# Experts of the first layer store their outputs as rows of a table, and the second layer gathers two rows for each token

## The chip, the core and the metric

One core of a Trainium2 chip runs the kernel. The metric is the device time of one execution in microseconds (us). The kernel before has a median of 1223.6 us over three runs (1219.67 to 1224.37).

## The reference

A two-layer diffusion backbone works on 512 latent tokens and 256 context tokens, each of 1024 numbers. Layer 0 mixes tokens by gated linear attention beside dense attention, layer 1 by windowed attention (128 tokens to each side, and the context). Behind each mixer stands a mixture of 16 experts, two of which are chosen for each token. The part that matters here, cut down:

```
x, ctx = x + gate2 * mixer(...)             # layer 0, then layer 1
tok  = concat(modulate(x), modulate(ctx))   # layer 0: 768 tokens; layer 1: the 512 latent ones
combine[n, e] = weight of expert e for token n, nonzero for two e
f    = sum over e of (silu(tok @ Wg[e]) * (tok @ Wu[e]) * combine[:, e]) @ Wd[e]
x    = x   + gate5_latent  * f[:512]        # gate5: one row of 1024 numbers each
ctx  = ctx + gate5_context * f[512:]        # layer 0 alone
```

Layer 1 begins with a root-mean-square norm and a modulation of x and ctx and their projection to queries, keys and values.

## The kernel before

**Tokens and experts.** The 768 tokens are six tiles of 128 rows. Tiles 4 and 5 are the context; they are worked on first (order 4, 5, 0, 1, 2, 3; "tile 0" and so on below count in this order). A router gives every token and choice a place among the 128 slots of its expert (`CAP`). Where an expert has more tokens than slots, a branch after the experts (`overflow`) does the rest; it is not taken here. `H` in device memory holds the modulated tokens, `F` the residual stream, written by the mixer.

**One expert.** POOL gathers its 128 rows of `H` by an indirect DMA into `hg` (L1026). PE transposes them (`hgtr`), ACT and DVE split them into a high and a low part (`hh`, `hlo`). The weights stream in on SP's hardware queue (L112) into a ring of buffers, are split by ACT (`whi`, L205) and DVE (`wlo`, L206), and PE makes three products for each (`eacc`). ACT and DVE form `sg`, PE transposes it (`hidtr`), ACT copies it (`th`, L1068), and PE makes the expert's output in two halves of 512 columns (`yacc`). An expert's `yacc` stands one step behind its `eacc`. The order on each engine follows the order in which `between`, `expert_up` and `expert_down` call each other.

**What becomes of an output in layer 0.** DVE makes the gate row of each slot, context or latent (`expert_gate`, L1076), and multiplies both halves of `yacc` by it (L1091). POOL adds the rows into `F` by an indirect DMA with addition (L1093); rows of empty slots lie out of bounds and are skipped, so 768 x 2 = 1536 of the 2048 slot rows are written. Layer 1's experts do the same into the output, with one gate row for all.

**The start of layer 1.** The tiles of `F` are loaded by SP (`xc`, L1665; three buffers). The first load waits for all additions into `F`. The other tiles, and the query weights (`uq`, 4 units of 512 KB in two loads each, `wraw<-in_od_w_in_dram`, L317), wait until the first load has landed. For each tile ACT squares and sums, POOL takes the power (`ss`, L211, L212), DVE scales (`xn`, L781), PE transposes (`xtr`), ACT and DVE make the halves of the modulated tile (`tf`, L795 and L797) and split it (`hT` and `hL`; `hT1c` and `hL1c` for the context). PE then projects it (`acc`): 256 columns for keys and values (weights loaded earlier) for each tile, and 512 columns of queries for the latent tiles with `uq`, which ACT and DVE split first (`whi`, `wlo`, 128x1024).

Of the kernel before, what the change touches and what calls it, by code (L numbers as in the profile page):

```python
# [18 lines left out]
P = 128  # L19
D = 1024  # L20
# [127 lines left out]
class K:  # L148
# [65 lines left out]
    def setup(self):  # L214
        nc = self.nc
        self.cpool = self.pool("cpool")
        self.cb = self.cpool.tile([P, NCONST], F32, name="cb")
        self.ident = self.cst("ident")
        self.mhalf = self.cpool.tile([P, 32], F32, name="mhalf")
        nc.vector.memset(self.mhalf, -0.5)  # L220
        self.ring = self.pool("ring", bufs=5)
        self.dram = self.pool("dram", space=DRAM)
        self.rowstack = ExitStack()
        self.rowp = self.pool("rowp", stack=self.rowstack, side="right")
        self.modT = [self.cpool.tile([P, 2, 16], F32, name=f"modT{l}") for l in range(2)]
        self.modD = [self.dram.tile([2, 6 * D], F32, name=f"modD{l}") for l in range(2)]

# [676 lines left out]
    def route_tiles(self, l, T, wk):  # L904
# [4 lines left out]
        r["ws"], r["idx"] = t("ws", [P, 16]), t("idx", [P, 2, 16], U32)  # L909
        r["ctx"] = t("ctx", [P, 16])  # L910
        r["counts"] = t("counts", [P, 2, P], F32R)
# [5 lines left out]
    def route_group(self, wk, pt, ix, L, n0, G, r):  # L917
# [42 lines left out]
        if last:  # L960

            r["done"] = V.tensor_scalar(r["idx"][:, 0, :], ix[:, :16], float(NOROW), float(T * P - 1), op0=ALU.add, op1=ALU.min).ins
            V.tensor_scalar(r["idx"][:, 1, :], ix[:, :16], float(NOROW), None, op0=ALU.add)
            V.tensor_scalar(r["ctx"], ix[:, :16], float(SEQ - NOROW), None, op0=ALU.is_ge)

# [41 lines left out]
    def route(self, wk, r, l):  # L1007

        V = self.nc.vector
        T = r["T"]  # L1010
        keep = wk.tile([P, 2, T], F32, name=f"keep{l}")
        V.tensor_scalar(keep, r["pos"], float(CAP), None, op0=ALU.is_ge)
# [57 lines left out]

    def expert_gate(self, e, gate, isctx, wk):

        if len(gate) == 1:
            return gate[0]
        y = wk.tile([P, D], F32, tag="y", name="y", bufs=2)
        self.nc.vector.scalar_tensor_tensor(y, gate[1], isctx[:, e:e + 1], gate[0], op0=ALU.mult, op1=ALU.add)  # L1076
        return y

    def expert_down(self, e, st, h, F, rows, gate, idx, wk, pm, adds):

        nc = self.nc
        y = wk.tile([P, D], F32, tag="yo", name="yo", bufs=2) if rows == SEQ else gate
# [9 lines left out]
        x = EORDER[e]  # L1092
        i = nc.gpsimd.indirect_dma_start(F, bass.IndirectOffsetOnAxis(ap=idx[:, 1, x:x + 1], axis=0), y, None,  # L1093
# [145 lines left out]
def emit(ctx, tc, A, out, dbg=None, upto=99):  # L1239
# [298 lines left out]
    def experts(l, T, F, st, r):  # L1538
# [20 lines left out]
        with s2:  # L1559
# [11 lines left out]
            sg = None  # L1571
            hid, slot_gate, adds = {}, {}, []

            def between(e, sg):
# [3 lines left out]
                if e == 0:  # L1578
                    k.slot_weights(r, pt)
                else:  # L1580
                    slot_gate[e - 1] = k.expert_gate(EORDER[e - 1], gate, r["ctx"], ew)
                if e + 1 < NEXP:
# [4 lines left out]
            for e in range(NEXP + 1):  # L1587
# [4 lines left out]
                if e > 0:  # L1592
                    k.expert_down(e - 1, st, hid[e - 1], F, T * P, slot_gate[e - 1], idx, ew, pm, adds)
        return n
# [19 lines left out]
    op = k.pool("oT1", stack=so)  # L1614
    oh, ol = op.tile([P, 8, SEQ], F32R, name="oh1"), op.tile([P, 8, SEQ], F32R, name="ol1")
    s0, sh, sn, sp = ES(), ES(), ES(), ES()
# [30 lines left out]
    with ES() as s1:  # L1647
# [14 lines left out]
        first = None  # L1662
        for i in order:
# [44 lines left out]
    def q_rest():  # L1708
        yield from k1
        qacc = pm.tile([P, 2, 256], F32, name="qacc")  # L1710
        for v in range(2):
            u = k.proj_units(hk, [(0, k.cols(W, 768, 256))], 256, w=256) if v else u1
            for i in range(4):
                acc = qacc[:, i % 2, :]
                for j in range(4):
# [3 lines left out]
                    yield  # L1719

    V = lambda kt, v: zk[:, kt, 128 + 64 * v:192 + 64 * v]
    blocks = []
# [48 lines left out]
```

## Time and profile before

| | |
|---|---|
| median of three runs | 1223.6 us (1219.67 to 1224.37) |
| the profiled execution | 1226.32 us, of which the span is 1224.6 us |
| mean granted clock of TensorE | 0.952 |
| busy share PE / DVE / ACT / POOL | 90% / 65% / 50% / 19% |
| chain that ended last | PE 57%, DVE 8%, DMA 8%, ACT 4%, POOL 4%, issue 3% |

All times in the rows below are microseconds from the start of the span, or durations, unless the view says ns. PE is the matrix engine (PEld its weight loads), DVE, ACT and POOL the vector, scalar and GpSimd engines; SP only issues DMAs. A name such as `F<-y,idx` is output<-input. The chain of waits follows the work that ended last back from what released it. Layer 0's experts run from about 565 to 731 us; layer 1's projections from there to about 801.

### The profile page before, as it was taken

The page shows a single profiled execution, that of the slowest core. Times are in us where ns is not written, and L with a number is a line of the kernel's source. Part 1 is how long each engine was busy: PE and PEld are TensorE (multiplying, and loading weights), DVE is VectorE, ACT ScalarE, POOL GpSimd, SP SyncE. Part 2 cuts the span into 40 slices and gives each one's busy share as a digit, 9 for nine tenths or more (in the row PEclk, how much of TensorE's full clock was granted, in tenths as well). Part 3 has the DMA queues.
Part 4 walks back from the last instruction along what each step waited for, and adds up shares of the span by engine and source line. Part 5 has one row for each costly group of instructions (what it writes and reads, how often), then busy time and mean ns, then how long its engine had stood idle before and what let it go on. Part 6 is the DMA issues. An engine that isn't in the chain of part 4 may idle for free.

```text
span 1224.6 us, 21495 instructions
## 1 busy us (share of the span) xinstructions
PE 1105.9 (90%) x7986; PEld 817.4 (67%) x7986; DVE 791.5 (65%) x1613; ACT 614.4 (50%) x1266; POOL 237.2 (19%) x252
## 2 busy tenths in 40 slices
PE   5999998998889989978999885989989996899996
PEld 2688887665556667866777654877766785677773
DVE  2532355677677753668888765677688447677773
ACT  3533644555466652216555536467588522555551
POOL 1000011224222000031222221331230004133321
PEclk8999999999899999978999996999999998899998
DMA  9711102776464428658999977012041374998992
GB/s 319 238 47 60 35 11 82 272 235 214 170 224 131 148 86 262 223 207 283 348 326 333 325 233 227 12 44 70 1 138 36 108 256 174 314 318 289 297 308 46
DMA packets 106251, 228.11 MB, mean 186 GB/s; under 512 B 21429, under 2 KB 30391, under 8 KB 106132
## 3 DMA queue, kind: packets, MB, share of 16 engines
q1 hardware_dynamic: 94324, 197.15, 48.0%
q0 software_dynamic: 9216, 22.09, 7.3%
q10 hardware_dynamic: 2592, 7.34, 1.5%
q8 instruction: 67, 1.10, 0.4%
q14 instruction: 52, 0.43, 0.1%
HBM read 210.60 MB, written 27.41 MB: 194 GB/s over the span
## 4 chain that ended last, share of the span: by engine, by line
PE 57%; DVE 8%; DMA 8%; ACT 4%; POOL 4%; issue 3%; SPq 1%; POOLq 0%; ACTq 0%; DVEq 0%
PE eacc L172 11%; PE acc L172 11%; PE yacc L172 7%; PE ptr L184 4%; DMA wraw<-in_exp_w_up_dram 4%; PE pv L172 4%; PE sc L172 4%; PE modps L172 3%; PE qacc L172 3%; PE hgtr L184 2%; PE co L172 2%; PE lg L172 2%; POOL rq L435 1%; DVE wlo L206 1%; PE h2tr L184 1%
## 5 line engine op out<-in xcount | busy, mean ns | idle before, releaser
L206 DVE TENSOR_TENSOR wlo<-wraw,whi 128x1024 fp32r<-128x1024 f32 (+2 forms) x184 | 210.2, 1156 | 80.9 <-ACT whi L205 71.0
L205 ACT CAST whi<-wraw 128x1024 fp32r<-128x1024 f32 (+2 forms) x184 | 181.1, 994 | 145.4 <-PE eacc L172 94.8
L172 PE MATMUL eacc<-whi,hh 128*128 128x512 f32 x256 | 119.7, 468 | 0.0
L172 PE MATMUL yacc<-wraw,th 128*128 128x512 f32 x256 | 115.2, 593 | 1.1 <-ACT th L1068 1.1
L172 PE MATMUL eacc<-whi,hlo 128*128 128x512 f32 x256 | 102.6, 401 | 0.0
L172 PE MATMUL eacc<-wlo,hh 128*128 128x512 f32 x256 | 102.2, 399 | 0.0
L172 PE MATMUL acc<-whi,hT 128*128 128x512 f32 (+2 forms) x256 | 91.8, 359 | 4.8 <-ACT hT L205 4.8
L172 PE MATMUL acc<-wlo,hT 128*128 128x512 f32 (+2 forms) x256 | 88.8, 347 | 0.5 <-DVE wlo L206 0.4
L184 PE MATMUL ptr<-cb,P 128*128 128x128 f32 x480 | 77.5, 284 | 12.8 <-ACT PT L540 6.4
L172 PE MATMUL acc<-whi,hL 128*128 128x512 f32 (+2 forms) x256 | 88.4, 345 | 0.0
L172 PEld LDWEIGHTS yacc<-wraw,th 128*128 128x128 f32 x256 | 48.2, 189 | 49.9 <-issue 44.1
L184 PEld LDWEIGHTS ptr<-cb,P 128*128 128x128 f32 x480 | 52.9, 141 | 38.8 <-ACT PT L540 9.9
L172 PE MATMUL modps<-mw,csT 128*32 128x512 f32 (+1 forms) x448 | 64.8, 571 | 10.4 <-DMA mw<-in_mod_w_dram 6.1
L172 PE MATMUL sc<-Kst,Qh 128*128 128x512 f32 (+2 forms) x192 | 64.7, 344 | 3.6 <-ACT P L544 3.5
L504 DVE CUSTOM_DVE_ANT_0 sc<-sc,mk,sink 128x512 f32<-128x512 f32 (+1 forms) x64 | 56.2, 882 | 16.8 <-PE sc L172 14.6
L540 ACT COPY PT<-ptr 128x512 f32<-128x512 f32 x96 | 56.1, 587 | 16.8 <-PE ptr L184 15.7
L172 PE MATMUL pv<-PT,z_k 128*64 128x256 f32 x480 | 63.7, 389 | 0.0
L172 PEld LDWEIGHTS eacc<-whi,hh 128*128 128x128 f32 x256 | 49.9, 195 | 14.5 <-issue 6.7
L172 PEld LDWEIGHTS eacc<-wlo,hh 128*128 128x128 f32 x256 | 50.0, 195 | 14.3 <-issue 6.7
L172 PEld LDWEIGHTS acc<-whi,hT 128*128 128x128 f32 x256 | 49.4, 193 | 14.5 <-ACT hT L205 5.2
L172 PE MATMUL sc<-Kst,Ql 128*128 128x512 f32 (+2 forms) x192 | 56.5, 316 | 1.1 <-DVE Ql L206 1.1
L172 PEld LDWEIGHTS eacc<-whi,hlo 128*128 128x128 f32 x256 | 49.3, 192 | 11.9 <-DVE hlo L206 0.7
(331 smaller groups left out, 2530.7 us busy)
## 6 DMA issues: line engine op xcount, KB each, us to landing
mw<-in_mod_w_dram SPq DMA_DIRECT2D x80, 512.0 KB
wraw<-in_exp_w_gate_dram SPq DMA_DIRECT2D x128, 256.0 KB
wraw<-in_exp_w_up_dram SPq DMA_DIRECT2D x128, 256.0 KB
wraw<-in_exp_w_down_dram SPq DMA_DIRECT2D x64, 512.0 KB
mw<-in_mod_w_dram SPq DMA_DIRECT2D x32, 256.0 KB
wraw<-in_ev_w_in_dram SPq DMA_DIRECT2D x12, 512.0 KB
wraw<-in_od_w_in_dram SPq DMA_DIRECT2D x20, 256.0 KB
wraw<-in_od_w_out_dram SPq DMA_DIRECT2D x16, 256.0 KB
```

The lines of the kernel that those rows point to most:

```text
L172: return self.nc.tensor.matmul(out, lhsT=l, rhs=r, start=start, stop=stop)
L184: self.nc.tensor.transpose(out, in_, self.ident[:in_.shape[0], :in_.shape[0]])
L205: self.nc.scalar.copy(hi, src)
L206: self.nc.vector.tensor_tensor(lo, src, hi.bitcast(F32), op=ALU.subtract)
L435: nc.gpsimd.tensor_tensor(rq[:, 0, :], ms, self.mhalf[:, :8], op=ALU.pow)
L504: nc.vector.tensor_tensor_reduce(sc[:, lo:lo + L], sc[:, lo:lo + L], mask, rq[:, 1, h:h + 1], sink[:, 1, h:h + 1], ALU.add, ALU.min, mx[:, ...
L540: (nc.scalar.copy if a0 == 0 else nc.vector.tensor_copy)(u2["PT"][:, a0:a0 + m, j2, :], t[:, 0:m, :])
```

## The change

Layer 0's experts no longer gate and no longer add. Each expert's 128 output rows are copied out of PSUM unscaled (half 0 by ACT, half 1 by DVE) and written by a plain DMA on POOL's software queue to rows 128x to 128x+127 of a table `Y` in device memory, for all slots. The router works out for each token the two rows of `Y` that hold its outputs (`slot`; tokens over `CAP` point to a row of zeros). At the start of layer 1, POOL gathers two rows of `Y` for each token of a tile, and DVE adds the two, multiplies by the gate row and adds the result to the loaded tile of `F`; the four latent tiles are written back to `F` by ACT's queue. The two buffers for each of two tiles are the memory in which the attention output is kept later. What was released by the landing of the first `xc` load (the other tiles' loads and `uq`) is now released by the landing of tile 0's second gather, and so are tile 1's gathers. The gathers of tile t+2 wait until DVE has read tile t's buffers. Layer 1's experts keep their gate and their addition.

```diff
+        self.slot = self.cpool.tile([P, 2, 6], U32, name="slot")
+        self.Y = self.dram.tile([NEXP * P + 1, D], F32, name="Y")
...
+        if l == 0:
+            by = wk.tile([P, 2, T, 16], F32, name="slotby")
+            sl, far = (wk.tile([P, 2, T], F32, name=n) for n in ("slotf", "slotn"))
+            V.tensor_tensor(by, r["OH"], self.cst("iota")[:, None, None, 0:16].to_broadcast([P, 2, T, 16]), op=ALU.mult)
+            V.tensor_reduce(sl, by, axis=AX.X, op=ALU.add)
...
-    def expert_gate(self, e, gate, isctx, wk):
...
-        self.nc.vector.scalar_tensor_tensor(y, gate[1], isctx[:, e:e + 1], gate[0], op0=ALU.mult, op1=ALU.add)
...
+        x = EORDER[e]
+        if gate is None:
+            for n in range(2):
+                (nc.scalar.copy, nc.vector.tensor_copy)[n](y[:, n * 512:(n + 1) * 512], ya[n])
+            nc.gpsimd.dma_start(self.Y[x * P:(x + 1) * P, :], y)
+            return
...
-        gate = [k.row(cp, l, t, 5, f"g5_{t}") for t in range(T // 2 - 1)]
-        if T == 6:
-            with tc.issue_after(r["dve"]):
-                nc.vector.tensor_tensor(gate[1], gate[1], gate[0], op=ALU.subtract)
...
+        def fetch_y(t):
+            yi[t] = [spare(oh, 2 * (t % 2) + j) for j in range(2)]
+            return [nc.gpsimd.indirect_dma_start(yi[t][j], None, k.Y, bass.IndirectOffsetOnAxis(ap=k.slot[:, j, t:t + 1], axis=0)).ins
+                    for j in range(2)]
+        spare = lambda o, j: o[:, j, :]
+        for t, i in enumerate(order):
+            m = 0 if i < 4 else 1
             xi[i] = wk.tile([P, D], F32, tag="xc", name="xc", bufs=3)
-            d = nc.sync.dma_start(xi[i], F[i * P:(i + 1) * P, :]).ins
+            ds = [nc.sync.dma_start(xi[i], F[i * P:(i + 1) * P, :]).ins]
+            if m not in g5:
+                g5[m] = spare(ol, m)
+                nc.sync.dma_start(g5[m], k.modD[0][m, 5 * D:6 * D].partition_broadcast(P))
+            if t < 2:
+                ds += fetch_y(t)
             if first is None:
-                first = d
+                first = ds[2]
             else:
-                k.after(d, first)
+                for d in ds:
+                    k.after(d, first)
...
+                t = order.index(i)
+                ya, yb = yi[t]
+                nc.vector.tensor_tensor(ya, ya, yb, op=ALU.add)
+                nc.vector.tensor_tensor(ya, ya, g5[m], op=ALU.mult)
+                nc.vector.tensor_tensor(xi[i], xi[i], ya, op=ALU.add)
+                if t + 2 < 6:
+                    fetch_y(t + 2)
                 k.norm_hT(wk, pt, xi[i], AB1[:, m, :], k.modT[1][:, m, 0:8], *parts(i))
+                if i < 4:
+                    nc.scalar.dma_start(F[i * P:(i + 1) * P, :], xi[i])
```

The order of instructions moves with it. DVE before, from the end of the branch behind layer 0's experts (`C_q` to `S_k` are rotary tables):

```order
L1105 UNCONDITIONAL_BRANCH x2
L353 TENSOR_TENSOR C_q<-cs,gb_q 128x256
L359 TENSOR_TENSOR S_q<-cs,gb_q 128x8x16 x2
L353 TENSOR_TENSOR C_k<-cs,gb_k 128x256
L359 TENSOR_TENSOR S_k<-cs,gb_k 128x8x16 x2
L781 TENSOR_SCALAR xn<-xc,ss 128x1024 x2
L797 TENSOR_SCALAR tf<-xtr,AB_4100,modT_70 128x128 x4
L781 TENSOR_SCALAR xn<-xc,ss 128x1024
L206 TENSOR_TENSOR hL1c<-tf,hT1c 128x4x128 x2
```

DVE now, from the first instruction that does any work behind that branch (L1703 to L1705 are the three new operations of a tile; `early_oh` holds gathered rows, `early_ol` the gate rows):

```order
L1703 TENSOR_TENSOR early_oh_7861<-early_oh_7861 128x1024
L1704 TENSOR_TENSOR early_oh_7861<-early_oh_7861,early_ol_7862 128x1024
L1705 TENSOR_TENSOR xc<-xc,early_oh_7861 128x1024
L1703 TENSOR_TENSOR early_oh_7861<-early_oh_7861 128x1024
L1704 TENSOR_TENSOR early_oh_7861<-early_oh_7861,early_ol_7862 128x1024
L1705 TENSOR_TENSOR xc<-xc,early_oh_7861 128x1024
L206 TENSOR_TENSOR wlo<-wraw,whi 128x1024 x2
L783 TENSOR_SCALAR xn<-xc,ss 128x1024
L206 TENSOR_TENSOR wlo<-wraw,whi 128x1024 x2
L799 TENSOR_SCALAR tf<-xtr,AB_4102,modT_70 128x128 x4
L206 TENSOR_TENSOR hL1c<-tf,hT1c 128x4x128
L783 TENSOR_SCALAR xn<-xc,ss 128x1024
```

The rotary tables stand ahead of the branch now. Tile 0's `xn` stands behind both first tiles' new operations and two of the four splits of the query weights, and its `tf` behind all four; before, no split stood ahead of either. Of the twelve new operations of the other four tiles, eight stand ahead of the first latent tile's `tf`.

SP before, its loads from the first tile of `F` on (`cs` is the table's constants):

```order
L1665 DMA xc<-F 128x1024
L346 DMA cs<-in_consts_dram 128x512
L1665 DMA xc<-F 128x1024 x3
L317 DMA wraw<-in_od_w_in_dram 128x2x256
L1665 DMA xc<-F 128x1024
L317 DMA wraw<-in_od_w_in_dram 128x2x256
L1665 DMA xc<-F 128x1024
L317 DMA wraw<-in_od_w_in_dram 128x2x256 x11
```

SP now, from the same load:

```order
L1684 DMA xc<-F 128x1024 x3
L319 DMA wraw<-in_od_w_in_dram 128x2x256 x11
L1684 DMA xc<-F 128x1024
L319 DMA wraw<-in_od_w_in_dram 128x2x256 x2
L1684 DMA xc<-F 128x1024 x2
```

The eight loads of the query weights are the first eight `wraw` rows of both lists; now they all stand ahead of the fourth tile's load.

## Rows read from the trace of the kernel before

**Rows 1.** The page, busy time of each engine over the span.
```profile
PE 1105.9 (90%) x7986; PEld 817.4 (67%) x7986; DVE 791.5 (65%) x1613; ACT 614.4 (50%) x1266; POOL 237.2 (19%) x252
```
**Rows 2.** Windows in layer 0's experts: us, busy by engine (count), PEclk, DMA share, GB/s.
```profile
605.00:625.00 20.00, 20.00 (x85) 14.06 (x84) 17.40 (x20) 11.28 (x17) 5.08 (x5) 1.00 0.96 322
645.00:665.00 20.00, 20.00 (x86) 14.06 (x85) 17.29 (x20) 10.72 (x16) 5.17 (x4) 1.00 0.99 333
```
**Rows 3.** Chain of waits in layer 0's experts: start, us, what.
```profile
577.40 3.43 PE yacc L172 x8
...
617.69 3.43 PE yacc L172 x8
...
625.32 9.71 DMA wraw<-in_exp_w_gate_dram
...
688.24 10.28 DMA wraw<-in_exp_w_up_dram
...
713.79 3.43 PE yacc L172 x8
...
727.14 3.71 PE yacc L172 x8
```
**Rows 4.** Chain of waits from there into layer 1.
```profile
730.88 0.70 DVE y L1091
...
731.84 6.33 DMA F<-y,idx
738.25 3.43 DMA xc<-F
741.73 3.47 DMA xc<-F
```
**Rows 5.** DVE, the start of layer 1 (timeline).
```profile
744.02 0.75 DVE L781 TENSOR_SCALAR xn<-xc,ss 128x1024 f32<-128x1024 f32 x1
...
748.13 1.36 DVE L797 TENSOR_SCALAR tf<-xtr,AB,modT 128x128 f32<-128x128 f32 x4
...
754.48 1.21 DVE L206 TENSOR_TENSOR wlo<-wraw,whi 128x1024 fp32r<-128x1024 f32 x1
...
762.34 1.22 DVE L206 TENSOR_TENSOR wlo<-wraw,whi 128x1024 fp32r<-128x1024 f32 x1
```
**Rows 6.** PE, the first latent tile's projection (timeline).
```profile
762.85 0.58 PE L172 MATMUL acc<-whi,hT 128*128 128x256 f32 x1
```
**Rows 7.** Windows from the first tile of layer 1 to the end of its projections.
```profile
741.00:763.00 22.00, 13.20 (x77) 11.36 (x77) 14.98 (x31) 17.03 (x33) 5.63 (x12) 0.73 0.79 263
763.00:785.00 22.00, 22.00 (x130) 19.16 (x130) 14.23 (x34) 12.29 (x32) 5.58 (x10) 0.94 0.08 23
785.00:801.00 16.00, 16.00 (x95) 13.79 (x94) 11.42 (x30) 8.03 (x20) 6.94 (x9) 1.00 0.06 14
```
**Rows 8.** DMA queues, 622 to 700 us: packets, MB, share of 16 engines.
```profile
q1 hardware_dynamic: 9272, 20.05, 70.9%
q0 software_dynamic: 2061, 5.65, 28.2%
```
**Rows 9.** DVE by shape, 560 to 735 us: busy us, mean ns | idle before.
```profile
L1091 DVE TENSOR_TENSOR y<-yacc,y 128x512 f32<-128x512 f32 x32 | 20.8, 681 | 1.6 <-PE yacc L172 1.4
L1076 DVE SCALAR_TENSOR_TENSOR y<-g,ctx,g 128x1024 f32<-128x1024 f32 x16 | 20.4, 1278 | 0.0
```
**Rows 10.** ACT in a steady expert (timeline; in brackets the idle time before).
```profile
602.39 1.05 ACT L205 CAST whi<-wraw 128x1024 fp32r<-128x1024 f32 x1 [3.49 <-PE eacc L172]
```
**Rows 11.** ACT by shape, 560 to 735 us.
```profile
L205 ACT CAST hh<-hgtr 128x512 fp32r<-128x512 f32 x30 | 16.0, 584 | 2.1 <-PE hgtr L184 2.1
```
**Rows 12.** Chain of waits, the first expert's gather.
```profile
552.38 4.49 DMA hg<-H,idx
```
**Rows 13.** Line L1026: ns min/median/max, first and last start.
```profile
L1026 POOL DMA_INDIRECT hg<-H,idx x32: 937/1043/2050, 552.4 to 1172.8; - x32
```
**Rows 14.** Line L882, a plain operation of the new ones' shape.
```profile
L882 DVE TENSOR_TENSOR h<-h,B x6: 1212/1224/1226, 504.7 to 1022.7; 128x1024 f32<-128x1024 f32 x6
```

More of the change, by code (lines that the diff above doesn't have):

```diff
@@ L909, in route_tiles @@
         r["ws"], r["idx"] = t("ws", [P, 16]), t("idx", [P, 2, 16], U32)
-        r["ctx"] = t("ctx", [P, 16])
         r["counts"] = t("counts", [P, 2, P], F32R)
@@ L963, in route_group @@
             V.tensor_scalar(r["idx"][:, 1, :], ix[:, :16], float(NOROW), None, op0=ALU.add)
-            V.tensor_scalar(r["ctx"], ix[:, :16], float(SEQ - NOROW), None, op0=ALU.is_ge)
         def total():
@@ L1010, in route @@
         T = r["T"]
+        if l == 0:
[3 more added lines that the diff above has]
+            V.tensor_reduce(sl, by, axis=AX.X, op=ALU.add)
+            V.scalar_tensor_tensor(sl, sl, float(P), r["pos"], op0=ALU.mult, op1=ALU.add)
+            V.tensor_scalar(far, r["pos"], float(CAP), float(2 * NEXP * P), op0=ALU.is_ge, op1=ALU.mult)
+            V.tensor_tensor(sl, sl, far, op=ALU.add)
+            V.tensor_scalar(self.slot, sl, float(NEXP * P), None, op0=ALU.min)
         keep = wk.tile([P, 2, T], F32, name=f"keep{l}")
@@ L1069, in expert_hid @@
         return th
-    def expert_gate(self, e, gate, isctx, wk):
-        if len(gate) == 1:
-            return gate[0]
-        y = wk.tile([P, D], F32, tag="y", name="y", bufs=2)
-        self.nc.vector.scalar_tensor_tensor(y, gate[1], isctx[:, e:e + 1], gate[0], op0=ALU.mult, op1=ALU.add)
-        return y
     def expert_down(self, e, st, h, F, rows, gate, idx, wk, pm, adds):
         nc = self.nc
-        y = wk.tile([P, D], F32, tag="yo", name="yo", bufs=2) if rows == SEQ else gate
+        y = wk.tile([P, D], F32, tag="yo", name="yo", bufs=2)
         ya = [pm.tile([P, 512], F32, tag="mm", name="yacc") for _ in range(2)]
@@ L1545, in experts @@
         cp = k.pool(f"gates{l}", stack=s2)
-        gate = [k.row(cp, l, t, 5, f"g5_{t}") for t in range(T // 2 - 1)]
-        if T == 6:
-            with tc.issue_after(r["dve"]):
-                nc.vector.tensor_tensor(gate[1], gate[1], gate[0], op=ALU.subtract)
+        gate = None
+        if l == 1:
+            gate = k.row(cp, l, 0, 5, "g5")
+        else:
+            none = cp.tile([8, P], F32, name="none")
+            nc.gpsimd.memset(none, 0.0)
+            nc.gpsimd.dma_start(k.Y[NEXP * P:NEXP * P + 1, :].rearrange("o (p j) -> (o p) j", p=8), none)
         ny = NY[l]
@@ L1571, in experts @@
             sg = None
-            hid, slot_gate, adds = {}, {}, []
+            hid, adds = {}, []
             def between(e, sg):
@@ L1579, in between @@
                     k.slot_weights(r, pt)
-                else:
-                    slot_gate[e - 1] = k.expert_gate(EORDER[e - 1], gate, r["ctx"], ew)
                 if e + 1 < NEXP:
@@ L1592, in experts @@
                 if e > 0:
-                    k.expert_down(e - 1, st, hid[e - 1], F, T * P, slot_gate[e - 1], idx, ew, pm, adds)
+                    k.expert_down(e - 1, st, hid[e - 1], F, T * P, gate, idx, ew, pm, adds)
         return n
@@ L1614, in emit @@
     op = k.pool("oT1", stack=so)
-    oh, ol = op.tile([P, 8, SEQ], F32R, name="oh1"), op.tile([P, 8, SEQ], F32R, name="ol1")
+    oh, ol = [op.tile([P, 4, D], F32, tag=n, name=f"early_{n}", bufs=1) for n in ("oh1", "ol1")]
     s0, sh, sn, sp = ES(), ES(), ES(), ES()
@@ L1662, in emit @@
         first = None
-        for i in order:
-            xi[i] = wk.tile([P, D], F32, tag="xc", name="xc", bufs=3)
-            d = nc.sync.dma_start(xi[i], F[i * P:(i + 1) * P, :]).ins
+        g5, yi = {}, {}
+        def fetch_y(t):
[5 more added lines that the diff above has]
+            m = 0 if i < 4 else 1
+            xi[i] = wk.tile([P, D], F32, tag="xc", name="xc", bufs=3)
+            ds = [nc.sync.dma_start(xi[i], F[i * P:(i + 1) * P, :]).ins]
[4 more added lines that the diff above has]
+                ds += fetch_y(t)
             if first is None:
-                first = d
+                first = ds[2]
             else:
-                k.after(d, first)
+                for d in ds:
+                    k.after(d, first)
         tq, tk = k.rope_tables(zp, (("q", A["swa_q_norm"][0]), ("k", A["swa_k_norm"][0])), wk.tile([P, 4, P], F32, tag="tf", name="cs").rearrange("p a b -> p (a b)"))
@@ L1719, in q_rest @@
                     yield
+    oh, ol = [op.tile([P, 8, SEQ], F32R, tag=n, name=n, bufs=1) for n in ("oh1", "ol1")]
     V = lambda kt, v: zk[:, kt, 128 + 64 * v:192 + 64 * v]
```

1 line of the change is left out of this document (removed).

## The prediction

> **What bounds the kernel now.** I read the page's busy shares first: PE is at 90% [rows 1], so a change counts where PE waits or is made to. There are two such places near the change, and the windows and the chain of waits show them.
>
> The first is layer 0's experts. PE is busy in all 20 us of both windows, but the DMA share is 0.96 and 0.99 [rows 2]: two limits lie close together. The chain tells which ends last. From 577.40 to 617.69 it goes through PE's `yacc` four times, a step of 40.29/4 = 10.07 us. From 625.32 to 698.52 it goes through seven weight loads of 9 to 11 us (the first and the last stand in [rows 3]), (698.52 - 625.32)/7 = 10.46 us apart. Thirteen steps of 10.07 behind 577.40 an expert's `yacc` would start at 708.3; it starts at 713.79 [rows 3]. So late weights cost 5.5 us of stalls or stretched matmuls there.
>
> The second is the start of layer 1. The last `yacc` ends at 727.14 + 3.71 = 730.85 [rows 3]. Then come DVE's gating, the last addition into `F` (6.33 us until it has landed), and tile 0's load (3.43) [rows 4]; `xn` of tile 0 is at 744.02, its `tf` at 748.13, and the first latent tile's projection at 762.85 [rows 5, 6]. From there to 801 PE is busy without a gap (22.00 of 22.00, 16.00 of 16.00 [rows 7]). So whatever moves 762.85 moves all that follows.
>
> **The change part by part**, on the clock of the profiled execution (1226.32 us; the median of the runs is 2.7 below it).
>
> *DVE and ACT in the experts.* DVE loses sixteen gate rows (20.4 us) and half of 20.8 us of multiplications [rows 9]; ACT gains sixteen copies of 128x512, by the nearest cast of 0.584 each 9.3 us [rows 11]. DVE does not end last in a steady step, so its 30 us are worth nothing by themselves. ACT's copy falls into its idle 3.49 us ahead of the next cast [rows 10] and costs nothing; at the last expert, where ACT's `th` stands behind that copy and PE waits for it, I count 0.6.
>
> *DMA in the experts.* Between 622 and 700 us (16 engines, 1248 engine-us) the hardware queue takes 0.709 x 1248 / 20.05 = 44.1 engine-us for a MB, the software queue 0.282 x 1248 / 5.65 = 62.3 [rows 8]. The software queue carries gathers, which move whole rows as the weight loads do, and eight additions; I lay the excess on the additions: 18.2 x 5.65 / 16 = 6.4 us, 0.8 for each expert. The table takes all 128 slots in place of 1536/16 = 96: 32 rows of 4 KB, 0.131 MB x 44.1 / 16 = 0.36. Relief 0.44 for an expert, 5.7 over the thirteen: as much as the lag. I take -5.0. Bounds: -5.5 (the whole lag; behind it PE is the limit), and +4.6, if a plain write on that queue costs the queue's mean (0.131 x 62.3 / 16 = 0.51 for each of the nine late experts).
>
> *Routing.* Six small DVE operations come in and the subtraction of the gate rows (the shape of [rows 14], 1.22) goes; both within 1 us, opposite in sign: 0.
>
> *The last table write.* The trace has no plain write from POOL. From below it is bounded by the 3.43 us of SP's load of the same 512 KB, from above by the addition's 6.33 [rows 4]; the nearest is POOL's own plain move of 512 KB, the gather's 4.49 [rows 12]. I take 4.45: 1.9 less than before, so the tile 0 gathers can go at 738.25 - 1.9 = 736.35.
>
> By the Trainium skill ("DMA: Bandwidth & Descriptors", Anatomy of one DMA), such a DMA takes some 2.0 us and its bytes at 436 GB/s, an estimate of 3.2 us here and a sum 1.2 us smaller. The gather of this size took 4.49 [rows 12], so the trace stands above that rule.
>
> *Tile 0.* Its load of `F` waits for no expert any more and is hidden. Two gathers: the second goes 1.04 behind the first [rows 13] and takes 4.49: landed at 741.9. That is no earlier than the old load (741.68): the gathers eat what the shorter write gives. Three DVE operations of 1.224 [rows 14], 3.7 us: 745.6.
>
> *What 741.9 lets go.* Tile 1's two gathers (1.05 MB), two tiles of `F` (1.05 MB) and the eight query loads (2.1 MB) start together, 4.2 MB. The same stretch moved 263 GB/s [rows 7]: 16 us, 757.9. With the best of [rows 2], 333 GB/s, 12.6 us: 754.5. I take 15, 756.9, and half of that for tile 1's gathers, 749.4; its three operations end at 753.1. Queued behind them on DVE are two query splits and then tile 0's `xn`, so `xn` is at some 755.5 where it was at 744.02. Then come the other two splits, which need the last query weights: 756.9, ACT's cast and DVE's split (1.05 [rows 10] and 1.22 [rows 5]) and one more split in the queue, 760.4. Only then does tile 0's `tf` start, at 748.13 before: 12.3 later. Nothing covers this: PE has no other work ready, as it had none before.
>
> *From tile 0's `tf` to the first latent projection.* Before, 762.85 - 748.13 = 14.7 us, with four splits among the work (first and last in [rows 5], 4.9 us). Now the splits are done, and eight of the new operations stand in the queue there (9.8): 14.7 + 9.8 - 4.9 = 19.6. DVE was idle 22.00 - 14.98 = 7.0 us of that window [rows 7], so up to some 4 may be taken in. I keep 19.6, since POOL's power now stands behind gathers that wait for DVE: 760.4 + 19.6 = 780.0, 17.2 later than 762.85.
>
> *From there on* four more operations (4.9 us) meet a DVE that was busy 14.23 + 11.42 of 38 us [rows 7]: hidden. The write-back of four tiles (2.1 MB) meets a DMA share of 0.08 and 0.06 [rows 7]: hidden.
>
> Sum: -5.0 + 0.6 + 17.2 = +12.8, so 1239.1 on the profiled execution's clock and 1236.4 against the median. I say 1236.
>
> **The rivals.**
>
> *A heavier jam (slower still).* The gathers of tile 1 share the DMA engines evenly with everything let go with them and land with the last of it, at 757.9. Then tile 1's operations end at 761.6, four splits follow (4.9) and tile 0's `tf` starts at 766.5, 6.1 later than in my sum: 1242 to 1243. For it: `tf` waits for both. Against: SP issues its loads one after another and POOL's two need not wait for those at the back. Beside it, the Trainium skill ("DMA: Bandwidth & Descriptors", Issuing engines are not separate DMA queues) has all issuing engines' transfers interleave on the same 16 engines, which speaks for this rival; no row here shows a gather released together with a long row of loads.
>
> *No change.* The low ends together: the lag is gone whole (-5.5), the write takes 3.43 (-1.0), the pile-up moves at 333 GB/s (-2.4), DVE's 4 idle us take in work (-4): 12.8 - 0.5 - 1.0 - 2.4 - 4.0 = +4.9, so 1228.5. It needs all of these.
>
> *Faster.* The start of layer 1 is bound by the query weights and not by DVE. Before, the last query split at 762.34 [rows 5] stands directly ahead of 762.85 [rows 6]. They are now let go at the same point (741.9) minus the experts' gain (5.5), and stand ahead of the fourth to sixth tiles' loads in SP's queue. If the additions and gathers fit into the wait for the weights, the first latent projection comes 5 us earlier and the kernel takes 1223.6 - 5.5 - 1.0 = 1217. The point from which it decides: tile 1's gathers have to land by about 747.4, which is the 1.04 + 4.49 of two gathers alone, and DVE has to do eighteen operations (22 us) in a window of 22 us in which it was busy 15 [rows 7]. The second condition speaks plainly against it.
>
> *The experts get no lighter.* If the write of all slots costs what the additions did, the -5.0 falls away: 1241.5. The shares of [rows 8] do not tell gathers from additions.
>
> **How the numbers follow.** My sum 0.42; the jam 0.15; the experts no lighter 0.10; no change 0.20; faster 0.13. What a measurement can tell from no change is 0.5%, 6 us: same is 1217.5 to 1229.7. The jam, the heavier experts and nearly all of my case lie above; some of my case reaches down to it (0.03): slower 0.64, same 0.23, faster 0.13. For the range of 8 in 10 I leave out most of the faster case below and the worst of the jam together with heavier experts above: 1219 to 1247. The range of my case alone is 1229 to 1242.
>
> **What would show it.** Right: `yacc` of the fourteenth expert about 5 us earlier; the last table write lands some 4.5 us after its issue; PE's wait ahead of layer 1 grows from 20 to about 30 us; in DVE's rows tile 0's `xn` stands behind six new operations of 1.22 us and two splits, `tf` behind the last split; the first latent projection 38 us before the end of the projections as now, with PE busy throughout; nothing else in layer 1 changes length. Wrong: the experts' step is unchanged and the chain there still goes through weight loads (heavier experts); DVE idles at the start of layer 1 while query weights are on their way, and the first latent projection follows directly on their split (faster); tile 1's gathers land last of all that was let go (jam); or PE starves between latent tiles, when DVE and not PE bounds the projections too, a loss beyond my range.

## The result, and the profile after

The changed kernel takes 1243.3 us (median of 4 runs, 1239.09 to 1247.35); the kernel before took 1222.52 beside it. The ratio is 1.0161 [1.0139, 1.0183]: slower by 20.8 us in the medians, where +12.8 was forecast. The ratios here and below are formed over the fast runs alone, while a median counts every run of a kernel, so that those of e1_early and e9_weights_behind include one far slower run each. The profiled execution took 1242.35 us (before 1226.32), its span is 1240.6, its mean granted clock 0.948. The page's busy row is nearly that of [rows 1]; the loss is no engine's work:

```profile
PE 1101.2 (89%) x7986; PEld 814.7 (66%) x7986; DVE 788.6 (64%) x1602; ACT 624.7 (50%) x1282; POOL 236.6 (19%) x266
```

**The experts got lighter.** The second window of [rows 2] again, columns as there:

```profile
645.00:665.00 20.00, 20.00 (x85) 14.06 (x84) 14.03 (x17) 12.57 (x18) 3.25 (x4) 1.00 1.02 374
```

DVE falls from 17.29 to 14.03 us, and more bytes move (374 GB/s for 333). The queues between 622 and 700 us, as in [rows 8]:

```profile
q1 hardware_dynamic: 10449, 23.21, 80.1%
q0 software_dynamic: 2160, 6.95, 22.2%
```

The software queue carries 6.95 MB in place of 5.65 in less time of the engines: 0.222 x 1248 / 6.95 = 39.9 engine-us for a MB, where it was 62.3. The hardware queue stays near 44 (0.801 x 1248 / 23.21 = 43.1). The chain of waits (start, us, what):

```profile
574.68 3.43 PE yacc L172 x8
...
705.62 3.43 PE yacc L172 x8
...
719.48 3.71 PE yacc L172 x8
724.44 3.74 DMA Y<-yo
...
728.94 1.01 POOL early_oh L1676
...
730.25 5.10 DMA early_oh<-Y,slot
...
739.62 11.96 DMA wraw<-in_od_w_in_dram
...
755.55 0.73 DVE tf L799 x2
...
766.71 1.06 POOL early_oh L1676
...
769.26 1.80 POOL early_oh L1676
...
773.53 1.08 POOL early_oh L1676
```

From 574.68 to 719.48 no weight load is left in the chain (seven stood there before [rows 3]): up to the last expert PE alone sets the pace. The thirteen steps to 705.62 take 130.94, so 10.07 each, the step that [rows 3] had where it went through PE. From the first `yacc` (574.52 in PE's own rows) to the end of the last (723.18) it is 148.7 us, 153.6 before.

Behind 723.2 the chain is another one than in [rows 4]: table write, gather, sum, then a query weight load, and further down POOL's gather issues. The first latent projection starts at 780.20, 57.0 us behind the last `yacc`; before, 762.85 - 730.84 = 32.0. PE's row for it, as in [rows 6]:

```profile
780.20 0.56 PE L172 MATMUL acc<-whi,hT 128*128 128x256 f32 x1
```

The difference of the two spans is 16.0 us: -2.7 (the first `yacc` starts at 574.52, before at 577.24, see below), -4.9 (experts), +25.0 (57.0 - 32.0), -1.4 (from the first latent projection to the end, 461.75 before and 460.4 now). The +25.0 divides at tile 0's rows: its data landed at +12.2 (before +10.8), its `tf` came 20.1 us later (6.5 before), the first latent projection 24.65 behind that (14.7 before).

Why `tf` is late stands in ACT's rows and DVE's (start, us, operation; in brackets the idle time before):

```profile
745.59 1.04 ACT L205 CAST whi<-wraw 128x1024 fp32r<-128x1024 f32 x1 [5.17 <-DMA wraw<-in_od_w_in_dram]
...
750.21 1.04 ACT L205 CAST whi<-wraw 128x1024 fp32r<-128x1024 f32 x1 [3.57 <-DMA wraw<-in_od_w_in_dram]
```

```profile
735.43 1.23 DVE L1703 TENSOR_TENSOR early_oh<-early_oh 128x1024 f32<-128x1024 f32 x1 [10.05 <-DMA early_oh<-Y,slot]
...
746.20 1.23 DVE L1703 TENSOR_TENSOR early_oh<-early_oh 128x1024 f32<-128x1024 f32 x1 [6.96 <-DMA early_oh<-Y,slot]
...
752.43 0.75 DVE L783 TENSOR_SCALAR xn<-xc,ss 128x1024 f32<-128x1024 f32 x1
753.27 2.36 DVE L206 TENSOR_TENSOR wlo<-wraw,whi 128x1024 fp32r<-128x1024 f32 x2
755.55 1.36 DVE L799 TENSOR_SCALAR tf<-xtr,AB,modT 128x128 f32<-128x128 f32 x4
...
771.71 0.75 DVE L783 TENSOR_SCALAR xn<-xc,ss 128x1024 f32<-128x1024 f32 x1 [1.55 <-POOL ss L212]
...
776.43 0.75 DVE L783 TENSOR_SCALAR xn<-xc,ss 128x1024 f32<-128x1024 f32 x1 [1.08 <-POOL ss L212]
...
777.46 1.22 DVE L1704 TENSOR_TENSOR early_oh<-early_oh,early_ol 128x1024 f32<-128x1024 f32 x1
778.59 1.36 DVE L799 TENSOR_SCALAR tf<-xtr,AB,modT 128x128 f32<-128x128 f32 x4
```

DVE waits 6.96 us for tile 1's gathers with tile 0's `xn` behind them, then come the splits that need the query weights, and `tf` follows directly on the last of them, as the prediction's step had it. In the second part the first latent tile's (tile 2's) `xn` at 771.71 and the next tile's at 776.43 wait for POOL's power. POOL's rows say what it did instead:

```profile
747.70 1.89 POOL L1676 DMA_INDIRECT early_oh<-Y,slot  x1 [6.10 <-DVE early_oh L1703]
749.61 0.77 POOL L212 TENSOR_TENSOR ss<-ss,mhalf 128x1 f32<-128x1 f32 x1
...
766.71 1.69 POOL L1676 DMA_INDIRECT early_oh<-Y,slot  x1 [5.26 <-DVE xc L1705]
768.47 0.52 POOL L211 TENSOR_SCALAR ss<-ss 128x1 f32<-128x1 f32 x1
769.26 1.80 POOL L1676 DMA_INDIRECT early_oh<-Y,slot  x1 [0.27 <-issue]
771.08 0.59 POOL L212 TENSOR_TENSOR ss<-ss,mhalf 128x1 f32<-128x1 f32 x1
```

A power's two steps (L211, L212) stand behind and between gathers whose buffers DVE has not freed. Tile 0's power waits 6.10 us so, since the gather ahead of it needs tile 1's first operation. That wait costs nothing here: tile 0's `xn` at 752.43 follows directly on a query split and has no wait for POOL. It is the powers of tiles 2 and 3 for which DVE waits (1.55 and 1.08 us).

### The profile page after: what moved, and what is told of

Read it like the earlier page. It is cut to its first block, busy times and chain, and to the rows that moved or that the text cites. A ratio compares the mean times of both kernels' runs of the same rounds, so it can differ in the third digit from the quotient of the medians.

```text
span 1240.6 us, 21538 instructions
## 1 busy us (share of the span) xinstructions
PE 1101.2 (89%) x7986; PEld 814.7 (66%) x7986; DVE 788.6 (64%) x1602; ACT 624.7 (50%) x1282; POOL 236.6 (19%) x266
## 4 chain that ended last, share of the span: by engine, by line
PE 62%; DVE 9%; POOL 4%; ACT 4%; DMA 3%; issue 3%; SPq 0%; POOLq 0%; ACTq 0%; DVEq 0%
PE eacc L172 14%; PE acc L172 11%; PE yacc L172 9%; PE ptr L184 4%; PE pv L172 4%; PE sc L172 4%; PE modps L172 3%; PE qacc L172 3%; PE hgtr L184 2%; PE co L172 2%; PE lg L172 1%; POOL rq L437 1%; DMA wraw<-in_od_w_in_dram 1%; PE h2tr L184 1%; ACT P L546 1%
## 5 line engine op out<-in xcount | busy, mean ns | idle before, releaser
L172 PEld LDWEIGHTS acc<-whi,hT 128*128 128x128 f32 x256 | 49.4, 193 | 14.4 <-ACT hT L205 5.2
L172 PEld LDWEIGHTS eacc<-whi,hh 128*128 128x128 f32 x256 | 48.9, 191 | 14.3 <-issue 6.7
L172 PEld LDWEIGHTS eacc<-wlo,hh 128*128 128x128 f32 x256 | 49.0, 191 | 14.1 <-issue 6.7
```

The lines of the kernel that those rows point to most:

```text
L172: return self.nc.tensor.matmul(out, lhsT=l, rhs=r, start=start, stop=stop)
```

## The experiments

The offsets from the end of the last `yacc` (E), in us of the profiled executions, tell more than starts do, since the first `yacc` itself starts anywhere from 572.75 (e5) to 578.51 (e2) in the six versions that have the changed kernel's code ahead of it, at 577.24 in before and at 579.80 in e4. So the 2.7 us by which it is earlier in after than in before lie within that spread.

| run | first `yacc` to E | first gather | tile 0's `xn` | tile 0's `tf` | first latent projection |
|---|---|---|---|---|---|
| before | 153.6 | - | 13.2 | 17.3 | 32.0 |
| after | 148.7 | 5.8 | 29.2 | 32.4 | 57.0 |
| e1_early | 148.7 | 5.3 | 23.7 | 28.9 | 50.3 |
| e2_gather1 | 148.7 | 5.5 | 21.2 | 31.4 | 48.9 |
| e3_no_sum | 148.7 | - | 12.2 | 15.1 | 34.2 |
| e4_plain_write | 148.0 | - | 11.3 | 14.2 | 32.8 |
| e5_one_op | 148.7 | 7.2 | 27.2 | 31.4 | 49.4 |
| e6_order | 148.7 | 7.0 | 19.5 | 28.3 | 49.4 |
| e7_combined | 148.2 | 9.5 | 26.8 | 30.5 | 43.5 |
| e8_late_weights | 148.2 | 7.4 | 29.0 | 32.8 | 46.6 |
| e9_weights_behind | 148.2 | 7.3 | 20.3 | 26.0 | 39.8 |

**e3_no_sum**: table as it is, but neither gathers nor sums.

```diff
-                ds += fetch_y(t)
...
-                first = ds[2]
+                first = ds[0]
+                k.after(first, k.lastY)
...
-                nc.vector.tensor_tensor(ya, ya, yb, op=ALU.add)
-                nc.vector.tensor_tensor(ya, ya, g5[m], op=ALU.mult)
-                nc.vector.tensor_tensor(xi[i], xi[i], ya, op=ALU.add)
```

> The experts of the changed kernel (copies and plain table writes) with the start of layer 1 as before: no gathers from the table, no sums, no write-back (the experts' outputs of layer 0 are left out of the result); tile 0's load of F waits for the last table write. Theory A: the experts' gain of the changed kernel stays whole (last yacc at 719 to 720 instead of 727.1) and the start of layer 1 takes the 32 us of before less 1.5 for the shorter write: 1213 to 1216 us. If the gain came from elsewhere (a luckier clock ahead of the experts): the experts take as long as before from the first gather to the last yacc, 174 to 175 us, and the kernel 1219 to 1222.

Measured: 1220.98 us, 0.997 [0.9953, 0.9988]. The expectation of 1213 to 1216 was missed, and the reason lies in its own sum. It took the earlier start of the experts in the profile of after (2.7 us) for a gain of the change; the spread of these starts shows that it need not be one. And the start of layer 1 is 34.2 us long, not 30.5. The table write explains little of that: it took 5.23 us, 1.1 less than the addition, where 1.5 less was counted. Its row of the chain:

```profile
725.14 5.23 DMA Y<-yo
```

Tile 0's `tf` is even 2.2 us earlier than before (15.1 for 17.3); the rest is lost behind it, 19.1 us to the first latent projection for 14.7 before. There the first latent tile's `tf` stands on DVE behind and between the last three query splits (753.04 to 756.85), and e4 has the same (18.6); what makes these late was not tried. What stands: the experts take 148.7 us as in after, and of the 57.0 us gathers and sums, with the write-back and the other release, make 57.0 - 34.2 = 22.8.

**e4_plain_write**: the kernel before, gating and all, whose experts write plainly in place of adding.

```diff
+        if rows != SEQ:
+            self.lastY = nc.gpsimd.dma_start(self.Y[x * P:(x + 1) * P, :], y).ins
+            return
...
+                k.after(first, k.lastY)
```

> The kernel before, with gate rows and gating on DVE as they were, but the indirect addition into F replaced by a plain write of all 128 rows into a table that nobody reads (the experts' outputs of layer 0 are left out of the result); tile 0's load of F waits for the last write. If the additions' DMA cost made the experts' weights late: the same as e3_no_sum within 1.5 us, and the last yacc at 719 to 721. If it was DVE's work (31 us less in the changed kernel): the last yacc at 725 or later, and 1219 to 1222.

Measured: 1217.52 us, 0.9945 [0.9917, 0.9972]; the experts take 148.0 us. The expected start of the last `yacc`, 719 to 721, was missed (724.14), as was the time of e3 within 1.5 us: the experts start late in this trace, at 579.80. Their length decides, 5.6 us less than before, and 148.0 to 148.7 in all ten versions without the additions. DVE's work is that of before, so these us come from the additions in the DMA and not from DVE. Its software queue between 622 and 700 us:

```profile
q0 software_dynamic: 2128, 6.78, 22.0%
```

Again 0.220 x 1248 / 6.78 = 40.5 engine-us for a MB. Laying the whole excess of [rows 8] on the additions was sound, and the rival that the experts get no lighter falls.

**e1_early**: the weights and the other tiles' loads are let go when tile 0's load of `F` has landed, not when its gathers have, and tile 1's gathers wait for the table alone.

```diff
-                first = ds[2]
+                first = ds[0]
...
-                for d in ds:
-                    k.after(d, first)
+                k.after(ds[0], first)
```

> The changed kernel, but what waited for tile 0's second gather (the other tiles' loads of F, the query weights) now waits for tile 0's load of F alone, which no expert writes, and tile 1's gathers wait for nothing but the table. Theory A (what the landing of the second gather lets go piles up, and tile 0 stands behind it in DVE's queue): the query weights land before tile 0's gathers, tile 0's first tf moves from 755.5 to about 745, the first latent projection from 780.2 to about 768 to 771, and the kernel takes 1231 to 1235 us. Theory B (the eighteen operations and twelve gathers are too much work by themselves, whenever they are let go): the first latent projection stays at 777 or later, 1240 or more.

Measured: 1235.91 us, 1.0076 [1.0055, 1.0098], 11.4 above the kernel before beside it, so about 9 us of the 20.8 go: a little less than the one theory's 1231 to 1235. That theory had `tf` some 10 us earlier and the projection 9 to 12; it is 3.5 and 6.7. The weights come earlier, but tile 0's gathers now share the DMA with them and land later, as DVE's row shows, 14.8 us behind E (12.2 in after):

```profile
741.56 1.23 DVE L1702 TENSOR_TENSOR early_oh<-early_oh 128x1024 f32<-128x1024 f32 x1 [12.60 <-DMA early_oh<-Y,slot]
```

Behind the sums POOL's power comes late, since a gather issue (748.11, 1.69 us) still stands between its two steps (747.38 and 749.82).

**e2_gather1**: only tile 1's gathers are freed from the wait for tile 0's second gather; the loads of `F` and the query weights keep it.

```diff
-                for d in ds:
-                    k.after(d, first)
+                k.after(ds[0], first)
```

> The changed kernel, but tile 1's two gathers no longer wait for tile 0's second; the loads of F and the query weights still do. Theory A with the query weights as what lands last: tile 1's operations end some 5 us earlier (745), but tf of tile 0 still stands behind the last query split, so it moves by 1 to 3 us only and the kernel takes 1240 to 1242. The jam of the prediction (tile 1's gathers are what lands last): tf moves by 6 us or more, 1236 to 1237.

Measured: 1239.02 us, 1.0102 [1.0051, 1.0152]. Tile 0's `xn` comes 8 us earlier, its `tf` only 1: it stands behind the weights' splits in either case, so the jam's gathers are not what holds it. Yet the first latent projection comes 8 us earlier, more than the one theory gave, because `tf` is not all: behind it tile 2's `xn` stands at 44.3 us behind E (48.5 in after) and its `tf` at 47.2 (55.4), and no gather stands between the two steps of its power (770.45 and 770.87). The four runs spread widely (1232.67 to 1241.7).

**e5_one_op**: one of the three new DVE operations per tile.

```diff
-                nc.vector.tensor_tensor(ya, ya, yb, op=ALU.add)
-                nc.vector.tensor_tensor(ya, ya, g5[m], op=ALU.mult)
-                nc.vector.tensor_tensor(xi[i], xi[i], ya, op=ALU.add)
+                nc.vector.tensor_tensor(xi[i], ya, yb, op=ALU.add)
```

> The changed kernel with one DVE operation for each tile instead of three (the tile is the sum of the two gathered rows; the residual and the gate are left out of the result). All loads, gathers and their order of release stay. Theory A (the last query split, which waits for its weights, holds tile 0's tf; only the five operations left out behind it count): the first latent projection moves from 57.0 us behind the last yacc to 50 to 52, 1236 to 1238 us. Theory B (DVE's work is the loss, all nine or ten operations left out ahead of that projection count): 45 to 47 us behind it, 1231 to 1233.

Measured: 1234.13 us, 1.0085 [1.0057, 1.0112]. `tf` moves by 1.0 us, the first latent projection by 7.6 to 49.4, between the numbers of the two theories (50 to 52 and 45 to 47). Two thirds of the new DVE work are worth 7.6 of the 25.0 us, or 9.0 if one counts from the first gather, which went 1.4 us later in this trace (7.2 for 5.8).

**e6_order**: the next gathers are issued behind a tile's `xn`, so that the power never stands behind them.

```diff
-                if t + 2 < 6:
-                    fetch_y(t + 2)
...
+                if t + 2 < 6:
+                    for d in fetch_y(t + 2):
+                        k.after(d, k.last_xn)
```

> The changed kernel, but the gathers of tile t+2 are issued behind tile t's norm (xn) and not behind its sums. POOL's power of tile 0 then has no gather of tile 3 ahead of it, and tile 0's xn comes ahead of tile 1's sums on DVE. No work is added or left out. If the order in the two queues costs (POOL's power behind gathers that wait for DVE): the first latent projection at 50 to 54 us behind the last yacc instead of 57.0, 1237 to 1240 us. If the order costs nothing because weights and work set the time: 56 us or more, 1242 to 1244; the later gathers could even cost 1 or 2.

Measured: 1241.03 us, 1.0125 [1.0098, 1.0153], 17.0 above the kernel before beside it, so some 4 us of the 20.8 go; 1237 to 1240 was expected. The first latent projection comes 7.6 us earlier, as it should if the order costs, and in the profiled execution (1246.28, the slowest of the four) all of it is given back: from there to the first attention scores it is 51.0 us, 43.2 in after. The gathers now come too late for the later tiles. A row of DVE, and one of PE:

```profile
785.13 1.23 DVE L1703 TENSOR_TENSOR early_oh<-early_oh 128x1024 f32<-128x1024 f32 x1 [5.11 <-DMA early_oh<-Y,slot]
```

```profile
796.26 1.09 PE L184 MATMUL xtr<-cb,xn 128*128 128x128 f32 x8 [3.48 <-DVE xn L783]
```

DVE waits 5.11 us for tile 4's gathers with tile 3's `tf` behind them, and PE then 3.48 us for tile 4's `xn`. Half of what is given back goes with the clock. The windows from the first latent projection to the first scores, e6 and then after, columns as in [rows 2]:

```profile
776.20:827.19 50.99, 43.59 (x235) 36.93 (x235) 35.25 (x77) 21.83 (x52) 17.30 (x27) 0.90 0.27 95
```

```profile
780.20:823.40 43.20, 39.72 (x232) 34.20 (x231) 31.53 (x70) 21.72 (x52) 13.98 (x20) 0.97 0.17 59
```

PE idles 3.9 us more, and its own work takes 3.9 us more at a mean granted clock of 0.90 for 0.97. POOL's order was one wait, the late gathers the next.

**e7_combined**: four tiles' gathers have buffers of their own and go at once; the query weights and the loads of `F` wait for nothing; the gate goes back into the experts, which leaves two operations per tile; later sums and gathers stand behind an earlier tile's `xn`. The edit, cut down, against the changed kernel:

```diff
-            yi[t] = [spare(oh, 2 * (t % 2) + j) for j in range(2)]
+            yi[t] = [spare((oh, ol)[t % 4 // 2], 2 * (t % 2) + j) for j in range(2)]
...
-            if t < 2:
+            if t < 4:
...
+                with (tc.issue_after(xns[t - 2]) if t >= 2 else ES()):
+                    nc.vector.tensor_tensor(ya, ya, yb, op=ALU.add)
+                    nc.vector.tensor_tensor(xi[i], xi[i], ya, op=ALU.add)
```

> All remedies at once, a full result: the gate goes back to the experts (two DVE operations for each tile), the loads of F and the query weights wait for nothing, four tiles' gathers have buffers and go right behind the last table write, the later ones behind a norm, and the sums of tile t+2 come behind tile t's norm. Theory A: tile 0's tf at 18 to 20 us behind the last yacc (before 17.3, changed kernel 32.4), the first latent projection at 34 to 36 (before 32.0, changed kernel 57.0); with 5.5 us gained in the experts 1219 to 1223 us, at best 5 below the kernel before. Theory B (sums and gathers cost by their amount): the first latent projection at 42 us or more, 1228 or more.

Measured: 1226.9 us, 1.0032 [1.0013, 1.0051]. The gate in the experts costs nothing (148.2 us). Theory A was missed: `tf` is at +30.5 (18 to 20), the first latent projection at +43.5 (34 to 36), as theory B had it (42 or more), and the kernel lies 0.3% above before. What remains stands in its chain:

```profile
724.38 7.76 DMA Y<-y
...
737.48 7.90 DMA early_oh<-Y,slot
```

The table write, 3.74 in after, takes 7.76 beside the weight loads. The gather in the chain is tile 1's second; with 7.90 it is no slower than in after (8.3), but tile 0's second takes 7.5 for 5.10, now beside the other tiles' gathers and loads. The order costs here too. POOL has tile 1's first step ahead of tile 0's power and waits 2.43 us for tile 1's square (749.21), so tile 0's `xn` is at +26.8, though its sums end at +21.0.

**e8_late_weights**: as e7, but the weights wait for tile 0's gathers again, and their splits are ordered behind tile 1's `xn` (two units) and tile 2's (two units) on DVE.

```diff
-                first = ds[0]
+                first = ds[2]
...
+                if t >= 2 and len(uq) < 4:
+                    with tc.issue_after(xns[t - 1]):
+                        uq += k.proj_split(hl, rq[len(uq):len(uq) + 2])
```

> The combined kernel again, a full result, with the query weights let go by the landing of tile 0's second gather as in the changed kernel, but split behind tile 1's and tile 2's norms (two units each), so that only two splits stand ahead of tile 0's tf on DVE and none ahead of its xn. In the combined kernel the last table write took 7.8 us beside the early weights, and tile 0's second gather landed 18 us behind the last yacc. If that was the early weights' doing: the write takes 3.5 to 4.5 us, the gathers land 11.5 to 13 us behind the last yacc, tile 0's xn is 6 us earlier (21 instead of 26.8), the first latent projection at 37 to 40 instead of 43.5 us, and the kernel takes 1220 to 1224 us, at or a little below the kernel before. If DVE's sums or POOL's gathers set the pace: the first latent projection stays at 42 to 44 us, 1226 to 1228.

Measured: 1240.74 us, 1.0118 [1.0087, 1.015]; 1220 to 1224 was expected. The transfers came some 1 us later than hoped (the write took 5.66 us for 3.5 to 4.5, the gathers fed DVE at +14.0 for 11.5 to 13); most of the miss lies in the queues. ACT's rows:

```profile
748.45 1.04 ACT L205 CAST whi<-wraw 128x1024 fp32r<-128x1024 f32 x1 [6.05 <-DMA wraw<-in_od_w_in_dram]
750.65 1.04 ACT L205 CAST whi<-wraw 128x1024 fp32r<-128x1024 f32 x1 [1.16 <-DMA wraw<-in_od_w_in_dram]
751.61 1.05 ACT L801 ACTIVATE xn<-xc 128x1024 f32<-128x1024 f32 x1
```

and POOL's:

```profile
752.83 0.21 POOL L211 TENSOR_SCALAR ss<-ss 128x1 f32<-128x1 f32 x1 [9.53 <-ACT xn L801]
753.12 1.40 POOL L212 TENSOR_TENSOR ss<-ss,mhalf 128x1 f32<-128x1 f32 x2
```

ACT's casts of the weights stand ahead of tile 1's square, so they wait for the weights there; POOL has tile 1's L211 ahead of tile 0's power, waits 9.53 us, and so tile 0's `xn` waits for a weight load that it doesn't need: it starts at +29.0, the sums end at +16.5.

**e9_weights_behind**: as e8 in all its work and transfers; only the casts and splits go behind tile 0's modulated halves (two units) and tile 1's (two units), and a tile's square goes behind the power before it.

```diff
-                if t >= 2 and len(uq) < 4:
-                    with tc.issue_after(xns[t - 1]):
+                if t in (2, 3):
+                    with tc.issue_after(sps[t - 2][0]), tc.issue_after(sps[t - 2][1]):
...
+                with (tc.issue_after(k.last_pow) if t else ES()):
```

> The same work as e8_late_weights, a full result, with nothing but the order in the queues changed: ACT's casts and DVE's splits of the query weights come behind tile 0's (first two units) and tile 1's (last two) modulated halves, and POOL's power of tile 0 ahead of tile 1's sum. In e8_late_weights the casts stood ahead of tile 1's square on ACT and waited for the weights until 748 to 751 us, and tile 0's power stood behind tile 1's sum on POOL: xn of tile 0 at 29 us behind the last yacc, though its sums were done at 16.5. If the order is what it cost: xn of tile 0 at 19 to 21, the first latent projection at 37 to 41 (46.6 there, 32.0 before), the kernel 1220 to 1226 us. If the late weights themselves set the time: the first latent projection at 44 us or later and 1232 or more.

Measured: 1227.39 us, 1.0024 [1.0004, 1.0043], 13 us less than e8. `xn` at 20.3 and the first latent projection at 39.8 lie where they would if the order is the cost; the time is 1.4 us above the 1220 to 1226 that went with them. DVE's rows:

```profile
737.23 1.23 DVE L1735 TENSOR_TENSOR early_oh<-early_oh 128x1024 f32<-128x1024 f32 x1 [11.89 <-DMA early_oh<-Y,slot]
...
743.45 0.75 DVE L803 TENSOR_SCALAR xn<-xc,ss 128x1024 f32<-128x1024 f32 x1 [0.47 <-POOL ss L212]
...
749.10 1.36 DVE L819 TENSOR_SCALAR tf<-xtr,AB,modT 128x128 f32<-128x128 f32 x4
```

`xn` comes 6.2 us behind the first sum's start, 17.0 in after. No version that does the whole work beat the kernel before: the two best, e7 and e9, lie 0.2 to 0.3% above it.

## Why the prediction was right in direction and short in size

**Experts: right.** -5.0 and the 0.6 make -4.4, measured -4.9. The additions were the load, as e4 shows by itself. The 0.6, PE's wait behind ACT's copy at the last expert, is there too: 148.7 us with that copy, 148.0 and 148.2 without it.

**Table write and tile 0's gathers: right within 1.2 us.** From E to landed gathers 11.05 forecast, 12.2 measured. The write was nearer to its lower bound (3.74; 3.43 to 6.33, 4.45 taken); the second gather was issued 1.3 behind the first and took 5.10 (1.04 and 4.49 taken). That the write came so near is partly luck: with the same code up to there it took 4.95 in e6 and 5.14 in e5.

**From landed gathers to tile 0's `tf`: right within 1.6.** 18.5 forecast, 20.1 measured, with the order that was named: tile 1's sum, two splits, `xn`, the last splits, `tf`. The splits ended on the last query weight, 16.2 us behind the release at 735.4 (15 forecast). e2 shows that this and not tile 1's gathers sets `tf`.

**"From tile 0's `tf` to the first latent projection": the step that was too small.** 19.6 forecast, 24.65 measured, 5.05 of the 7.3 us by which the sum falls short (12.8 forecast, -4.9 + 25.0 = 20.1 in the profiled executions). I had counted eight operations, and eight there are. But I let DVE's idle time pay for POOL's power behind the gathers, without working that wait out, and left out that more of the later tiles' other work now stands ahead of that projection too. The windows from `tf` to the projection, before and after, columns as in [rows 2]:

```profile
748.13:762.85 14.72, 11.11 (x69) 9.64 (x69) 11.84 (x24) 12.91 (x25) 3.88 (x8) 0.85 0.79 256
```

```profile
755.55:780.20 24.65, 12.41 (x68) 11.40 (x69) 19.47 (x34) 10.38 (x24) 10.62 (x12) 0.64 0.62 207
```

DVE works 7.6 us longer there, where 4.9 was counted (9.8 - 4.9), and idles 2.3 us longer (5.2 for 2.9), where nothing was counted: together the 5 us that were missing. In the chain that stretch goes through POOL alone from 766.71 to 777.2, and three gather issues take 4.6 us of it (1.69, 1.80 and 1.08): the first step of tile 2's power starts at 768.47 behind the gather of 766.71, the second at 771.08 behind another, and `tf` of that tile, at 778.59, stands on DVE behind tile 3's `xn`, which waits for its power too, and an operation of tile 4. PE waits 5.7 us for tile 2's `xn` and 5.0 for that `tf`:

```profile
PE xtr L184 <- ACT whi L205: 30.1, 1, 30.1
PE xtr L184 <- DVE xn L783: 5.7, 1, 5.7
PE xtr L184 <- DVE tf L799: 5.0, 1, 5.0
```

The 30.1 is PE's one long wait ahead of tile 0; it was 14.1 before. The forecast's "from 20 to about 30 us" fits neither it nor its own sum of +17.2: all of PE's idle time from E to the first latent projection was 19.0 before and is 42.7 now.

**From there on: hidden, as forecast.** To the end 460.4 us, 461.75 before; the projections take 38 us as before, with PE busy but for 0.1.

**The rivals.** The 1243.3 measured lie 1.3 us above the range that my own case had by itself (1229 to 1242); the range of 8 in 10 (1219 to 1247) holds them. The jam's time, 1242 to 1243, is nearly the one that came, but by another way, so by chance. Tile 1's gathers fed DVE at 746.20, 5.4 us before the last weight load landed (739.62 + 11.96), and e2 moved `tf` by 1 us. "Faster" asked that DVE's operations fit into the wait for the weights; e5 shows that they do not. "No change" needed DVE to take work in while it idled; it idled more (5.2 us for 2.9).

**What is shown and what is not.** Of the 25.0 us at the start of layer 1, 17.2 (57.0 - 39.8) go with another release, buffers for four tiles, another order and one operation less per tile, though two sums for each tile, the gathers and the table are all still there (e9). How the 17.2 divide among these isn't settled: e5, with two operations less, gained 7.6 in the old order, and e9 against e8, in which order alone differs, 6.8 at the first latent projection and 13 in the time (of the 12.1 between the two profiled executions 3.8 lie behind that projection and 1.6 ahead of E). The last 7.8 (39.8 - 32.0) I lay on the round trip through the table and the sums; that is argued, not shown. e3, with neither gathers nor sums, stands at 34.2, so that 5.6 of them lie between it and e9; which of gathers and sums holds more is open, since every version that took all sums out took the gathers out as well. Loading the query weights earlier into memory other than the ring was not tried.

## What to carry to other kernels

Moving a combination from scattered additions to a table takes load off the DMA where it was late, but puts write, gather and sum in a row at the one place where the next stage has nothing else to run: count that row before counting the relief. When work is put into a stage where several engines feed one another, its own duration is only a part: two of three operations left out gave 7.6 of 25.0 us (e5). Walk each in-order queue and ask, for every operation that waits for a DMA or for a buffer, which small critical operation stands behind it; e8 and e9 do the same work and lie 13 us apart.

## What was not expected of the hardware

- DMAs with addition cost the DMA engines 1.56 times as much for a MB in the software queue's mean (62.3 engine-us before, 39.9 and 40.5 without them); gathers share the queue, so an addition by itself costs more than that mean.
- POOL's issue of one indirect gather takes from 0.94 us (740.35 in after) to 1.89 (747.70), by no rule that these rows show. A busy DVE beside it does not settle it: 1.85 us at 735.61 and 0.95 at 737.77 both stand beside DVE's three operations on tile 0, which run from 735.43 to 739.24. The cause was not tried.
- The same 512 KB write to the table landed 3.74 us behind its issue in after, 4.95 in e6, 5.14 in e5 and 5.23 in e3, where hardly anything else moved beside it, and 7.76 beside weight loads (e7). So 1.5 us of difference need no neighbour.
- TensorE's granted clock falls where PE waits, and comes back when it is busy again. The windows of after, columns as in [rows 2]:

```profile
735.00:745.00 10.00, 0.00 (x0) 0.00 (x0) 3.67 (x3) 1.15 (x2) 4.99 (x5) 0.50 0.83 297
...
785.00:795.00 10.00, 10.00 (x62) 8.79 (x62) 6.19 (x10) 5.39 (x13) 3.11 (x6) 1.00 0.24 97
```

It is 0.50 (1.2 GHz) with PE idle and 1.00 (2.4 GHz) from 785 on. From E to the first latent projection PE's 77 instructions take 14.35 us, 13.05 before, at a mean of 0.60 for 0.73: some 1.3 us of the 25.0 may be the clock's. In e6 it is more (3.9 us behind the first latent projection).
